# A two-layer hybrid encoder on one core: a compact triangular inversion, group norm by scan step, and 512-column products in the feed-forward's output

## Chip, cores and metric

The kernel runs on 1 core of one Trainium2 chip. The metric is the device time of one execution in microseconds (us); lower is better. Engines are named as in the profile: PE (TensorE, with PEld its weight loads), DVE (VectorE), ACT (ScalarE), POOL (GpSimd) and SP (the engine that issues nearly all DMAs).

## The reference

An encoder of two layers over 256 tokens of width 1024, everything in float32. Each layer:

```python
for l in range(DEPTH):
    h = modulate(rmsnorm(x, norm_gains[l, 0]), sh1, sc1)
    x = x + 0.5 * gt1[:, None, :] * swiglu(h, ffn_wi[l, 0], ffn_wo[l, 0])
    h = modulate(rmsnorm(x, norm_gains[l, 1]), sh2, sc2)
    x = x + gt2[:, None, :] * hybrid_mixer(h, ...)
    h = modulate(rmsnorm(x, norm_gains[l, 2]), sh3, sc3)
    x = x + 0.5 * gt3[:, None, :] * swiglu(h, ffn_wi[l, 1], ffn_wo[l, 1])
return rmsnorm(x, final_norm)
```

The feed-forward's inner width is 2816, so its output product has 22 blocks of 128 to sum over. The shift, scale and gate vectors are `cs @ ada_w[l] + ada_b[l]`, a matrix of 1024 x 9216 per layer. The mixer sums three branches, each gated by a sigmoid: A (dilated attention), B (neighbourhood attention) and C, a recurrence with a state of 64 x 64 per head and direction:

```python
def _rwkv_step(state, inp):
    r, w, k, v, a_vec, b_vec = inp
    sa = jnp.einsum("dbhvk,dbhk->dbhv", state, a_vec)
    state = state * w[..., None, :] + sa[..., None] * b_vec[..., None, :] + v[..., None] * k[..., None, :]
    y = jnp.einsum("dbhvk,dbhk->dbhv", state, r)
    return state, y
...
yn = ((y - mean) * lax.rsqrt(var + GN_EPS)) * gn_w + gn_b        # group norm: one group per head and token
return (jnp.sum(yn + bonus, axis=0) * g)                        # the two directions summed, gated
```

## The kernel before

**Dense products.** Activations lie transposed (features on partitions, 256 tokens in the free dimension). Every float32 operand is split into two fp32r parts, hi and lo, and a product is three: hi·hi, hi·lo and lo·hi. `mm3` (lines 417 to 420) issues them for one 128 x 128 weight block, each with 256 columns: L418 (weights hi, activation hi), L419 (weights hi, activation lo), L420 (weights lo, activation hi). `dense` (L460) does that for all blocks of a sum into one half of a PSUM tile `pmain`, of which there are three. Weights arrive as float32 (`wraw`), ACT rounds a quarter of 512 columns to `whi` (L374) and DVE subtracts to get `wlo` (L383). One quarter holds four blocks, so it feeds twelve products, and four quarters can exist at once (`NSPL`).

**The feed-forward** (`ffn`, L784): 22 inner blocks `z` are made, then eight output blocks m, each a sum over 22 blocks: 176 weight blocks, 528 products of 256 columns. DVE adds each output block to x (`residual`, L609), and ACT and DVE prepare the next norm from it.

**The adaLN matrix** is read a block of 128 x 1024 at a time (`araw`) and reduced on DVE (L482), spread over the program; a block that has not landed holds up whatever stands behind it on DVE.

**Branch C** is done in four chunks of 64 tokens per direction: step n takes chunk n of the forward and chunk 3 - n of the backward direction, 8 heads each. For each step, `invert` (L1165) builds the chunk's masked Gram matrices G (`pG`, L1189) and inverts the unit triangular 64 x 64 matrices. `blocks8` (L1261) inverts the 8 x 8 diagonal blocks: it gathers them (L1270 to L1277), spreads them over the partitions by one product (`p`, L1283), runs a substitution of seven pairs of small DVE operations (L1288, L1292), each pair needing the one in front, and writes the result into 64 x 64 blocks (L1295). Two levels then join 8 x 8 to 16 x 16 and 16 x 16 to 32 x 32 blocks. Each level is a product `pX` = G·T (L1213), a copy to SBUF, a product `pT` (L1225), a masked copy on DVE (L1227) and a transpose of all 32 x 32 squares on DVE (`flip`, L1300). Each of these products is 16 matmuls of 64 x 64 with 64 columns. The third level (`corners`, L1258) is 16 matmuls of 32 x 32 that use the array's 32 x 32 tiles by `tile_position`. A plain float32 matmul shows as two records in the profile, so a group of 16 shows as x32.

`values` (L1302) makes the parts that need no inverse, and `scan` (L1352) runs the four steps in turn: `pAS`, `pU` (needs the inverse), `pS1` (the next state) and `pY`. `post` (L1454) is the group norm, the gate and the sum of directions; it is called for a direction and a half of the tokens, so it waits for two scan steps: the first two calls start after step 1, the last two after step 3. It squares (L1463), sums by a product (`pvar`, L1471), takes a root on ACT and a reciprocal on DVE, spreads it by transposes (`pgi`, L1489) and ends in `oC`, the hi and lo parts that branch C's output products read (L1512 to L1518).

**The order** of all engines' instructions is written down by a small list scheduler when the program is built (`Order`, lines 57 to 133). Pieces of work are generators with a priority; `on(engine, cost)` asks for an engine, and all that a generator issues between two such requests stays together on the engine. The main thread issues the dense products in the order of the weights (`ORDER` = "cabAgB", so branch A's output `A`, gates `g`, branch B's output `B`, then branch C's output), and the others go in between. Buffers are counted (`s_big`: 36 tiles of 4 KB per partition). The order is fixed at build time; on the chip an engine waits at an instruction whose operands are not there, and with it everything behind.

## Time and profile before

| | us |
|---|---|
| median of 3 runs | 1536.39 |
| lowest and highest | 1534.38, 1541.68 |
| the profiled execution | 1537.14 |
| its span in the profile | 1535.3 |

| engine | busy us | share of the span | instructions |
|---|---|---|---|
| PE | 1495.0 | 97% | 14470 |
| DVE | 1283.9 | 84% | 2731 |
| ACT | 859.4 | 56% | 1735 |

The profile is of one execution. Busy time of PE counts overlapping matmuls once; a matmul's record lasts longer than the step to the next one, so the pace is read from starts. The stages lie like this in the span: feed-forward 1 of layer 0 to 215 us, mixer to 589, feed-forward 2 to 779, feed-forward 1 of layer 1 to 970, mixer to 1338, feed-forward 2 to 1526, final norm to the end.

### The profile page before, as it was taken

What the parts mean: (1) busy time and instruction counts of PE and PEld (TensorE: products, weight loads), DVE (VectorE), ACT (ScalarE), POOL (GpSimd) and SP (SyncE); (2) the same over time, 40 slices, a digit from 0 to 9 for tenths busy, and PEclk for the clock granted to TensorE, in tenths of its full rate; (3) what the DMA queues carried; (4) which work ended last, traced back from release to release, by engine and by line L of the source; (5) the groups of instructions that cost most, each with busy time, mean ns of one, the idle gap of its engine ahead of it and who ended that gap; (6) DMA issues with size and microseconds to landing.
All of it is one profiled execution on the core that took longest, in us unless ns stands there. A gap on an engine that the chain in (4) does not pass through costs nothing.

```text
span 1535.3 us, 36372 instructions
## 1 busy us (share of the span) xinstructions
PE 1495.0 (97%) x14470; PEld 1424.6 (93%) x14470; DVE 1283.9 (84%) x2731; ACT 859.4 (56%) x1735; POOL 2.3 (0%) x22
## 2 busy tenths in 40 slices
PE   6999999999999989999999999999999998999998
PEld 6999999988888979999999999998888998999997
DVE  8889789989878888988789877899897888898664
ACT  4556466575444447555565545676655445665554
POOL 0000000000000000000000000000000000000000
PEclk9999999999999979999999999999999999999999
DMA  9688775525345645888668886644343456567553
GB/s 343 226 293 277 259 239 188 179 102 172 118 153 166 211 165 188 280 286 271 223 201 273 276 271 222 216 159 161 109 149 102 167 207 234 167 212 267 189 183 124
DMA packets 97377, 315.76 MB, mean 206 GB/s; under 512 B 11572, under 2 KB 23092, under 8 KB 97208
## 3 DMA queue, kind: packets, MB, share of 16 engines
q1 hardware_dynamic: 96920, 313.35, 60.8%
q8 instruction: 113, 1.85, 0.5%
q14 instruction: 56, 0.46, 0.1%
q10 hardware_dynamic: 288, 0.10, 0.0%
HBM read 310.27 MB, written 3.15 MB: 204 GB/s over the span
## 4 chain that ended last, share of the span: by engine, by line
PE 89%; DMA 5%; DVE 3%; issue 1%; SPq 1%; ACT 0%; DVEq 0%; ACTq 0%
PE pmain L418 21%; PE pmain L419 20%; PE pmain L420 20%; DMA araw<-in_ada_w_dram 3%; PE pearly L418 3%; PE pearly L420 2%; PE pearly L419 2%; DVE wlo L383 1%; PE pT L1225 1%; PE pX L1213 1%; PE pS L1568 1%; PE po L1608 1%; PE pfirst L419 1%; PE pmain L1724 1%; PE pfirst L420 1%; PE pfirst L418 1%
## 5 line engine op out<-in xcount | busy, mean ns | idle before, releaser
L374 ACT CAST whi<-wraw 128x512 fp32r<-128x512 f32 x828 | 508.1, 619 | 444.8 <-PE pmain L419 283.2
L383 DVE TENSOR_TENSOR wlo<-wraw,whi 128x512 fp32r<-128x512 f32 x828 | 567.1, 689 | 117.5 <-ACT whi L374 107.8
L418 PE MATMUL pmain<-h,whi 128*128 128x256 f32 x1840 | 530.5, 288 | 0.0
L419 PE MATMUL pmain<-h,whi 128*128 128x256 f32 x1840 | 517.6, 281 | 0.0
L420 PE MATMUL pmain<-h,wlo 128*128 128x256 f32 x1840 | 515.2, 280 | 0.6 <-DVE wlo L383 0.5
L418 PEld LDWEIGHTS pmain<-h,whi 128*128 128x128 f32 x1840 | 345.9, 188 | 13.9 <-issue 7.8
L420 PEld LDWEIGHTS pmain<-h,wlo 128*128 128x128 f32 x1840 | 347.2, 189 | 1.6 <-DVE wlo L383 1.4
L419 PEld LDWEIGHTS pmain<-h,whi 128*128 128x128 f32 x1840 | 346.5, 188 | 1.1 <-issue 0.7
L482 DVE CUSTOM_DVE_ANT_0 araw<-araw,csb 128x1024 f32<-128x1024 f32 x144 | 175.5, 1221 | 47.2 <-DMA araw<-in_ada_w_dram 46.9
L420 PE MATMUL pmain<-z,wlo 128*128 128x256 f32 x704 | 199.1, 283 | 5.6 <-DVE wlo L383 5.6
L419 PE MATMUL pmain<-z,whi 128*128 128x256 f32 x704 | 198.9, 282 | 0.0
L418 PE MATMUL pmain<-z,whi 128*128 128x256 f32 x704 | 198.1, 281 | 0.0
L420 PEld LDWEIGHTS pmain<-z,wlo 128*128 128x128 f32 x704 | 133.3, 189 | 6.8 <-DVE wlo L383 6.8
L418 PEld LDWEIGHTS pmain<-z,whi 128*128 128x128 f32 x704 | 133.3, 189 | 0.0
L419 PEld LDWEIGHTS pmain<-z,whi 128*128 128x128 f32 x704 | 133.3, 189 | 0.0
L418 PE MATMUL pearly<-xh,whi 128*128 128x258 f32 x320 | 91.4, 286 | 0.0
L419 PE MATMUL pearly<-xl,whi 128*128 128x258 f32 x320 | 90.4, 283 | 0.0
L420 PE MATMUL pearly<-xh,wlo 128*128 128x258 f32 x320 | 90.4, 282 | 0.0
L419 PEld LDWEIGHTS pearly<-xl,whi 128*128 128x128 f32 x320 | 60.6, 189 | 0.0
L420 PEld LDWEIGHTS pearly<-xh,wlo 128*128 128x128 f32 x320 | 60.5, 189 | 0.0
L418 PEld LDWEIGHTS pearly<-xh,whi 128*128 128x128 f32 x320 | 60.4, 189 | 0.0
L441 ACT CAST z<-ffz 128x256 fp32r<-128x256 f32 x76 | 30.6, 405 | 39.8 <-DVE ffz L673 39.7
(308 smaller groups left out, 2328.3 us busy)
## 6 DMA issues: line engine op xcount, KB each, us to landing
wraw<-in_ffn_wi_dram SPq DMA_DIRECT2D x160, 512.0 KB, 4.7
araw<-in_ada_w_dram SPq DMA_DIRECT2D x144, 512.0 KB, 6.5
wraw<-in_ffn_wo_dram SPq DMA_DIRECT2D x88, 512.0 KB, 4.6
wraw<-in_w_in_dram SPq DMA_DIRECT2D x78, 512.0 KB, 3.7
wraw<-in_w_gb_dram SPq DMA_DIRECT2D x72, 512.0 KB, 4.0
w0raw<-in_ffn_wi_dram SPq DMA_DIRECT2D x16, 512.0 KB, 10.9
wraw<-in_w_out_dram SPq DMA_DIRECT2D x16, 512.0 KB, 3.7
bt<-in_bt_dram SPq DMA_DIRECT2D x16, 192.0 KB, 4.4
```

Source lines behind the costliest of these rows:

```text
L374: S_.copy(hi, part(q))
L383: V.tensor_tensor(lo, part(q), hi, op=OP.subtract)
L418: P.matmul(o, w[0], xh, start=first, stop=False)
L419: P.matmul(o, w[0], xl, start=False, stop=False)
L420: P.matmul(o, w[1], xh, start=False, stop=last)
L441: S_.copy(self.hi(k), src)
L482: V.tensor_tensor_reduce(out=raw, in0=raw, in1=csb, scale=0.5, scalar=0.0, op0=OP.mult, op1=OP.add, accum_out=modT[l][:, blk:blk + 1])
L1213: P.matmul(px[half(h), d, h // 2], G[h % 2][half(h), d, h // 2, 0:64], T[half(h), d, h // 2], start=True, stop=True)
L1225: P.matmul(pt[half(h), d, h // 2], X[half(h), d, h // 2], TT[half(h), d, h // 2], start=True, stop=True)
L1568: P.matmul(pS[e][:, t], qT[half(e), hp, t * 128:(t + 1) * 128], kT[half(e), hp], start=True, stop=True)
L1608: P.matmul(po[half(e)], vv[:, j, (2 * hp + e) * 64:(2 * hp + e + 1) * 64], pr_[:, 2 * e + j], start=j == 0, stop=j == 1)
L1724: P.matmul(p[t], ha.hi(kk)[:, xs], wh, start=kk == 0, stop=False)
```

## The change

- **Compact blocks.** The two lower levels keep only the 32 x 32 diagonal squares of each 64 x 64 matrix: T, its transpose `Tt` and X are 128 x 256 instead of 128 x 512. A product of a level becomes `squares`: 32 matmuls of 32 x 32 with 32 columns on the four diagonal tiles of the array, instead of 16 of 64 x 64. The copies, masks and transposes of these levels have half the elements. Ahead of the third level two small operations (on ACT or DVE) spread `Tt` back into the 64 x 64 layout.
- **Substitution in one piece.** The gather and the substitution of `blocks8` are requested from DVE as a whole, so nothing is placed between their operations.
- **Group norm by step.** `pY` is copied into a tile of its own step, and `post` is called once per scan step for that step's two chunks. Two calls follow steps 0 and 1; the calls of steps 2 and 3 add their half and finish `oC`.
- **512 columns.** The hi and lo parts of `z` lie side by side, and one matmul with the hi weights streams both (512 columns) into the two halves of `pmain`; the lo weights follow with 256 columns. The halves are added to x one after the other (`residual2`).

```diff
@@ -446,6 +452,26 @@
+    class Pairs(Act):
+        def __init__(self, name, kt):
+            self.t = [big(name, (128, 2, 2, S), F32R) for _ in range(-(-kt // 2))]
+        def both(self, k):
+            return self.t[k // 2][:, k % 2].rearrange("p a b -> p (a b)")
...
@@ -467,6 +493,17 @@
+    def dense2(p, a, kt):
+        for k in range(kt):
+            yield from tl.next()
+            if a.ev[k].t is None or a.ev[k].t > od.cur.t:
+                yield wait(a.ev[k])
+            yield on("PE", MM, 0.0)
+            P.matmul(p, tl.last[0], a.both(k), start=k == 0, stop=False)
+            P.matmul(p[:, 0:256], tl.last[1], a.hi(k), start=False, stop=k == kt - 1)
...
@@ -612,6 +649,11 @@
+    def residual2(m, p, g, st):
+        yield on("DVE", 0.4, 0.0)
+        V.scalar_tensor_tensor(xT[:, m], p[:, 1], g[:, m:m + 1], xT[:, m], op0=OP.mult, op1=OP.add)
+        yield from residual(m, p[:, 0], g, st)
...
@@ -825,8 +867,8 @@
-            yield from dense(p[:, 0], za, NJ)
-            od.spawn(residual(m, p[:, 0], g, nst), 1)
+            yield from dense2(p.rearrange("p a b -> p (a b)"), za, NJ)
+            od.spawn(residual2(m, p, g, nst), 1)
...
@@ -1174,8 +1216,10 @@
-                    tx = big("tx", (128, 2, 2, 4, 64))
-                    T, X = tx[:, 0], tx[:, 1]
+                    tx = big("tx", (128, 1024))
+                    T, Tt, X = (tx[:, o:o + 256].rearrange("p (d h c) -> p d h c", d=2, h=4) for o in (0, 256, 512))
+                    m = tx[:, 512:1024].rearrange("p (d h c) -> p d h c", d=2, h=4)
+                    X2 = tx[:, 768:896].rearrange("p (h c) -> p h c", h=4)
...
@@ -1192,9 +1236,8 @@
-                yield from blocks8(G, X, TT)
-                yield on("DVE", 0.6)
-                flip(T, TT)
+                yield from blocks8(G, m, Tt)
+                flip(T, Tt)
...
@@ -1206,45 +1249,53 @@
-                    px = paux("pX", (128, 2, 4, 64))
+                    px = paux("pX", (128, 2, 4, 32))
-                    for d in range(2):
-                        for h in range(8):
-                            P.matmul(px[half(h), d, h // 2], G[h % 2][half(h), d, h // 2, 0:64], T[half(h), d, h // 2],
-                                     start=True, stop=True)
+                    squares(px, lambda d, i, b, k, c: G[b][k, d, i, c], lambda d, i, k: T[k, d, i])
-                        yield from copy_any(X, px, 512)
+                        yield from copy_any(X, px, 256)
-                        yield from copy_any(halves_(X, 0), halves_(px, 0), 256)
+                        yield from copy_any(halves_(X, 0), halves_(px, 0), 128)
-                    pt = paux("pT", (128, 2, 4, 64))
+                    pt = paux("pT", (128, 2, 4, 32))
-                    for d in range(2):
-                        for h in range(8):
-                            P.matmul(pt[half(h), d, h // 2], X[half(h), d, h // 2], TT[half(h), d, h // 2], start=True, stop=True)
-                    yield on("DVE", 0.335)
-                    V.copy_predicated(halves_(TT, 1), lvl[:, lv].rearrange("p d (x s) -> p d x s", s=w), halves_(pt, 1))
+                    squares(pt, lambda d, i, b, k, c: X[k, d, i], lambda d, i, k: Tt[k, d, i])
+                    yield on("DVE", 0.55)
+                    V.copy_predicated(halves_(Tt, 1), lvc[:, lv].rearrange("p d (x s) -> p d x s", s=w), halves_(pt, 1))
-                    yield on("DVE", 0.6)
-                    flip(T, TT)
+                    flip(T, Tt)
+                for r in range(2):
+                    yield on(("ACT", "DVE"), (0.37, 0.23))
+                    o, x = TT[:, :, :, 32 * r:32 * r + 32], Tt
+                    if od.cur.pick == "ACT":
+                        S_.activation(o, x, AF.Copy, scale=hm[:, r:r + 1])
+                    else:
+                        V.tensor_scalar(o, x, hm[:, r:r + 1], None, op0=OP.mult)
-                corners(px, lambda d, i, b, k, ca, cb: G[b][k, d, i, cb], lambda d, i, k, ca, cb: T[k, d, i, ca], 1)
-                X2 = X[:, 0, :, 0:32]
+                corners(px, lambda d, i, b, k, ca, cb: G[b][k, d, i, cb], lambda d, i, k, ca, cb: T[k, d, i], 1)
-                corners(pt, lambda d, i, b, k, ca, cb: X2[k, i], lambda d, i, k, ca, cb: TT[k, d, i, cb], 0)
+                corners(pt, lambda d, i, b, k, ca, cb: X2[k, i], lambda d, i, k, ca, cb: Tt[k, d, i], 0)
-                V.copy_predicated(skew(TT[:, 0, :, 32:64], TT[:, 1, :, 0:32]), lvl[:, 2].rearrange("p d (x s) -> p d x s", s=32),
+                V.copy_predicated(skew(TT[:, 0, :, 32:64], TT[:, 1, :, 0:32]), lvl.rearrange("p d (x s) -> p d x s", s=32),
+        def squares(p, w, x):
+            for d in range(2):
+                for i in range(4):
+                    for r in range(4):
+                        k, c = slice(32 * r, 32 * r + 32), slice(32 * (r % 2), 32 * (r % 2) + 32)
+                        P.matmul(p[k, d, i], w(d, i, r // 2, k, c), x(d, i, k), start=True, stop=True, tile_position=(32 * r, 32 * r))
...
@@ -1264,16 +1315,14 @@
+            yield on("DVE", 2.54)
-                yield on("DVE", 0.6, 0.0)
-            yield on("DVE", 0.74)
-            yield on("DVE", 0.6)
...
@@ -1282,18 +1331,16 @@
+            yield on("DVE", 3.2)
-                yield on("DVE", 0.13, 0.13)
-                yield on("DVE", 0.13, 0.13)
-            yield on("DVE", 0.6)
-            V.tensor_mul(by_k(TT), flat(tc8)[:, :, None, :].to_broadcast([128, 8, 8, 8]),
-                         m8[:, None, :, None].to_broadcast([128, 8, 8, 8]))
+            V.tensor_mul(TT.rearrange("p d h (k t) -> p (d h) k t", k=4), flat(tc8)[:, :, None, :].to_broadcast([128, 8, 4, 8]),
+                         m4[:, None, :, None].to_broadcast([128, 8, 4, 8]))
...
@@ -1407,12 +1454,11 @@
-                for d in range(2):
-                    yield from copy_any(RKV[d, 2][:, :, toks(cs[d])], p[:, d], 256)
-                    if n % 2 == 1:
-                        od.set(e_y[d, cs[d] // 2])
+                YS[n] = (W1, TT)
+                yield from copy_any(W1, p, 512)
-                free_big(5 - (n == 3))
+                od.set(e_y[n])
+                free_big(4 - (n == 3))
...
@@ -1451,53 +1497,45 @@
-        def post(d, t):
-            last = d != t
-            ts = slice(t * 128, (t + 1) * 128)
-            yield wait(e_y[d, t])
-            y = RKV[d, 2][:, :, ts]
-            sq = small2("gsq", (128, 4, 128))
+        def post(n):
+            last = n > 1
+            ts = [toks(n), toks(3 - n)]
+            both = lambda t: skew(t[:, :, ts[0]], t[:, :, ts[1]])
+            yield wait(e_y[n])
+            y, sq = YS[n]
+            sqt = sq.rearrange("p d h t -> p (d h t)").rearrange("p (h d t) -> p h d t", h=4, d=2)
+            S_.activation(sqt.rearrange("p h d t -> p d h t"), y, AF.Square)
+            flat = sqt.rearrange("p h d t -> p h (d t)")
+            yield on("PE", 0.9)
+                P.matmul(p[:, 2 * hp:2 * hp + 2], flat[:, hp], sel[:, 0, 0:2], start=True, stop=True)
-                V.tensor_mul(y, y, G1[0][:, :, ts])
+            yield on("DVE", 0.6)
+            V.tensor_mul(y, y, both(G1[0]))
+            yield on("DVE", 0.43)
+            V.tensor_copy(flat.rearrange("p a (b c) -> p (a b) c", b=2), r[:, :, None].to_broadcast([128, 8, 64]))
+            p = paux("pgi", (128, 4, 2, 64))
+            yield on("PE", 0.5)
+                P.transpose(p[:, hp].rearrange("p d t -> p (d t)"), flat[:, hp], ident)
+            pd = p.rearrange("p h d t -> p d h t")
+            b = both(bon[0])
+                yield on("DVE", 1.2)
+                V.tensor_mul(y, y, pd)
+                V.tensor_add(b, b, y)
-                V.tensor_mul(y, y, G1[0][:, :, ts])
+                od.set(e_z[n])
@@ -1505,25 +1543,26 @@
+                yield wait(e_z[3 - n])
+                h, lo = both(oC[0].h[0]), both(oC[0].l[0])
+                    yield on("DVE", 0.67)
+                    V.tensor_mul(y[:, :, sl], y[:, :, sl], pd[:, :, sl])
+                    V.tensor_add(y[:, :, sl], y[:, :, sl], b[:, :, sl])
+                    yield on("ACT", 0.264)
+                    S_.copy(h[:, :, sl], y[:, :, sl])
+                    V.tensor_tensor(lo[:, :, sl], y[:, :, sl], h[:, :, sl], op=OP.subtract)
+            free_big()
-                free_big(4)
+                free_big(2)
...
@@ -1664,9 +1703,8 @@
-            for d in range(2):
-                for t in range(2):
-                    od.spawn(post(d, t), 3)
+            for n in range(4):
+                od.spawn(post(n), 3)
```

Three places show how this moves instructions.

PE, at the end of layer 0's mixer (pY is the scan's last step, pvar and pgi the group norm, o is branch B's attention output, oC branch C's). Before:

```order
L420 MATMUL pmain<-o,wlo 128x256
L1471 MATMUL pvar<-c_sel,gsq 128x2 x8
L1489 MATMUL pgi<-c_ident,gsq 128x128 x8
L418 MATMUL pmain<-oC,whi 128x256
L419 MATMUL pmain<-oC,whi 128x256
```

Now:

```order
L1530 MATMUL pgi<-c_ident,tw 128x128 x4
L424 MATMUL pmain<-h,whi 128x256
L425 MATMUL pmain<-h,whi 128x256
L426 MATMUL pmain<-h,wlo 128x256
...
L426 MATMUL pmain<-o,wlo 128x256
L424 MATMUL pmain<-oC,whi 128x256
```

The first product of oC stood right behind the last pgi; now 102 dense products of 256 columns stand between them in layer 0, and 222 in layer 1 (before: 30 between the last two pgi groups, none behind the last). The last pvar and pgi are half as many.

PE, the third inversion of layer 1 (p is the spreading product of `blocks8`, pX the first level's product that needs the substitution's result). Before, from p on:

```order
L1283 MATMUL p_16392<-tx,c_b_115 128x512
L1378 MATMUL pU<-tw 64x64 x16
L418 MATMUL pmain<-h,whi 128x256
...
L1390 MATMUL pS_16449<-uv,bu 64x64 x16
```

Now, up to pX and behind it:

```order
L1332 MATMUL p_16227<-tx,c_b_118 128x512
L1417 MATMUL pAS<-st,ar 64x64 x16
L424 MATMUL pmain<-h,whi 128x256
...
L1298 MATMUL pX<-tx,G 32x32 x32
L1425 MATMUL pU<-tw 64x64 x16
L1298 MATMUL pT<-tx 32x32 x32
```

Before, pX of this step came after 66 dense products, pU, pS, pY, both pG groups and pvar; now pAS and 9 dense products stand between p and pX, and the scan's pU, pS and pY come between the levels.

DVE, the same inversion (w is the substitution's tile, araw the adaLN blocks). Before:

```order
L1288 TENSOR_TENSOR w_16316<-p_16392,w_16316 128x8x7
L1380 COPY uv<-pU 64x8x64
L1292 TENSOR_TENSOR w_16316<-w_16316 128x2x4x7
L383 TENSOR_TENSOR wlo<-wraw,whi 128x512
L1288 TENSOR_TENSOR w_16316<-p_16392,w_16316 128x8x6
L482 ISA araw,modT_124<-araw,csb 128x1024
```

Now:

```order
L389 TENSOR_TENSOR wlo<-wraw,whi 128x512
L519 ISA araw,modT_127<-araw,csb 128x1024
...
L1337 TENSOR_TENSOR w_16166<-p_16227,w_16166 128x8x7
L1340 TENSOR_TENSOR w_16166<-w_16166 128x2x4x7
...
L1340 TENSOR_TENSOR w_16166<-w_16166 128x2x4
L1342 TENSOR_TENSOR tx<-w_16166,m_113 128x256
L1347 STREAM_TRANSPOSE tx<-tx 128x256
```

The substitution no longer shares DVE with weight splits and adaLN blocks; here two adaLN blocks stand between the last wlo and it.

## Rows read from the trace of the kernel before

**Rows 1.** The page's busy time by engine: busy us, share, instructions.
```profile
PE 1495.0 (97%) x14470; PEld 1424.6 (93%) x14470; DVE 1283.9 (84%) x2731; ACT 859.4 (56%) x1735; POOL 2.3 (0%) x22
```
**Rows 2.** The page's chain that ended last, by engine.
```profile
PE 89%; DMA 5%; DVE 3%; issue 1%; SPq 1%; ACT 0%; DVEq 0%; ACTq 0%
```
**Rows 3.** The page's groups: count | busy, mean ns | idle before, releaser.
```profile
L374 ACT CAST whi<-wraw 128x512 fp32r<-128x512 f32 x828 | 508.1, 619 | 444.8 <-PE pmain L419 283.2
L383 DVE TENSOR_TENSOR wlo<-wraw,whi 128x512 fp32r<-128x512 f32 x828 | 567.1, 689 | 117.5 <-ACT whi L374 107.8
L420 PE MATMUL pmain<-z,wlo 128*128 128x256 f32 x704 | 199.1, 283 | 5.6 <-DVE wlo L383 5.6
```
**Rows 4.** Windows: us, PE, PEld, DVE, ACT, POOL busy (records), granted clock, DMA share, GB/s.
```profile
410.90:539.20 128.30, 127.32 (x2220) 114.81 (x2220) 106.79 (x227) 57.84 (x119) 0.00 (x0) 1.00 0.52 171
539.20:566.40 27.20, 19.91 (x123) 18.33 (x122) 21.92 (x52) 11.01 (x23) 0.00 (x0) 0.69 0.43 151
1155.80:1294.30 138.50, 138.42 (x2320) 126.14 (x2319) 112.05 (x241) 68.45 (x134) 0.00 (x0) 1.00 0.50 170
1294.30:1314.70 20.40, 15.62 (x103) 14.40 (x102) 19.32 (x47) 8.77 (x19) 0.00 (x0) 0.83 0.59 202
146.70:215.20 68.50, 65.07 (x531) 64.67 (x529) 55.16 (x105) 34.32 (x63) 0.93 (x7) 0.98 0.78 264
1463.30:1526.20 62.90, 62.90 (x532) 62.90 (x530) 34.57 (x59) 32.87 (x59) 0.00 (x0) 1.00 0.47 159
```
**Rows 5.** PE in time order, layer 0's mixer end: start, us, what, [idle <-releaser].
```profile
544.75 1.97 PE L1489 MATMUL pgi<-c_ident,gsq 128*128 128x128 f32 x8 [3.25 <-DVE gsq L1484]
550.11 0.58 PE L418 MATMUL pmain<-oC,whi 128*128 128x256 f32 x1 [3.40 <-ACT oC L1516]
```
**Rows 6.** PE in time order: pvar of an earlier half, full clock.
```profile
475.71 1.95 PE L1471 MATMUL pvar<-c_sel,gsq 128*128 128x2 f32 x16
```
**Rows 7.** PE in time order, layer 1's mixer end.
```profile
1294.68 0.66 PE L1489 MATMUL pgi<-c_ident,gsq 128*128 128x128 f32 x4 [0.17 <-DVE gsq L1484]
1296.74 0.38 PE L418 MATMUL pmain<-oC,whi 128*128 128x256 f32 x1 [1.41 <-ACT oC L1516]
```
**Rows 8.** PE: a third-level and a second-level group, the next group; L1258's records.
```profile
422.87 0.45 PE L1258 MATMUL pX<-tx,G 32*32 32x32 f32 x32
423.25 1.15 PE L1225 MATMUL pT<-tw,tx 64*64 64x64 f32 x32
424.33 0.45 PE L1258 MATMUL pT<-tw,tx 32*32 32x32 f32 x32
...
L1258 PE MATMUL pX<-tx,G x256: 191/191/212, 422.9 to 1271.2; 32*32 32x32 f32 x128
```
**Rows 9.** PE in time order: nine products of 512 columns (attention's values).
```profile
299.76 0.40 PE L1724 MATMUL pmain<-whi,h 128*128 128x512 f32 x1
...
301.87 0.28 PE L418 MATMUL pmain<-h,whi 128*128 128x256 f32 x1
```
**Rows 10.** Groups by line on DVE and ACT, columns as in rows 3.
```profile
L482 DVE CUSTOM_DVE_ANT_0 araw<-araw,csb 128x1024 f32<-128x1024 f32 x144 | 175.5, 1221 | 47.2 <-DMA araw<-in_ada_w_dram 46.9
L609 DVE SCALAR_TENSOR_TENSOR xT<-pmain,g,xT 128x256 f32<-128x256 f32 x48 | 23.1, 482 | 14.8 <-PE pmain L420 14.7
L443 DVE TENSOR_TENSOR z<-ffz,z 128x256 fp32r<-128x256 f32 x76 | 31.8, 421 | 1.8 <-ACT z L441 1.8
L1274 DVE TENSOR_REDUCE w<-tx 128x64 f32<-128x512 f32 x8 | 9.0, 1129 | 0.0
L1288 DVE TENSOR_TENSOR w<-p,w 128x56 f32<-128x56 f32 (+6 forms) x56 | 10.2, 187 | 0.3
L1380 DVE COPY uv<-pU 64x512 f32<-64x512 f32 x8 | 5.4, 674 | 1.0 <-PE pU L1378 0.9
L1382 ACT COPY uv<-pU 64x512 f32<-64x512 f32 x8 | 4.7, 582 | 7.0 <-DVE uv L1380 6.9
```
**Rows 11.** The chain that ended last, its end.
```profile
1526.34 0.49 DVE xT L609
```

More of the change, by code (lines that the diff above doesn't have):

```diff
@@ L273, in trunk @@
     sinT = const.tile([128, S], F32, name="sinT")
-    lvl = const.tile([128, 3, 2, 128], U8, name="lvl")
+    lvl = const.tile([128, 2, 128], U8, name="lvl")
+    lvc = const.tile([128, 2, 2, 64], U8, name="lvc")
+    m4, hm = (const.tile([128, n], F32, name=name) for n, name in ((4, "m4"), (2, "hm")))
     bsel = const.tile([128, 2, 2, 128], F32R, name="bsel")
@@ L447, in free, with hi, lo @@
             free_big(2 * self.n)
+    class Pairs(Act):
+        def __init__(self, name, kt):
+            self.n = -(-kt // 4)
+            self.t = [big(name, (128, 2, 2, S), F32R) for _ in range(-(-kt // 2))]
+            self.ev = [Event() for _ in range(kt)]
+        def hi(self, k):
+            return self.t[k // 2][:, k % 2, 0]
+        def lo(self, k):
+            return self.t[k // 2][:, k % 2, 1]
+        def both(self, k):
+            return self.t[k // 2][:, k % 2].rearrange("p a b -> p (a b)")
+        def free(self):
+            free_big(len(self.t))
     class Early:
@@ L469, in dense @@
             mm3(p, tl.last, a.hi(k), a.lo(k), k == 0, k == kt - 1)
+            tl.done()
+    def dense2(p, a, kt):
[6 more added lines that the diff above has]
+            P.matmul(p[:, 0:256], tl.last[1], a.hi(k), start=False, stop=k == kt - 1)
             tl.done()
@@ L763, in first_products @@
             if k == KT - 1:
-                yield take(s_big, 12)
-                za = Act("z", NJ)
+                yield take(s_big, 11)
+                za = Pairs("z", NJ)
             for i in range(NJ0 // 2):
@@ L795, in ffn @@
             od.spawn(modulated(l, n, st, ha), 0)
-            yield take(s_big, 12)
-            za = Act("z", NJ)
+            yield take(s_big, 11)
+            za = Pairs("z", NJ)
         for j in range(j0, NJ):
@@ L1347, in values @@
             if n_val[0] == 4:
-                free_big(4)
-        e_y = {(d, t): Event() for d in range(2) for t in range(2)}
+                free_big(6)
+        e_y, YS = [Event() for _ in range(4)], {}
         def scan():
@@ L1523, in post @@
                 od.release(s_px)
+            free_big()
             n_post[0] -= 1
             if n_post[0] == 0:
-                free_big(4)
+                free_big(2)
         half_done = [0] * 4
```

40 lines of the change are left out of this document (6 added, 34 removed).

## The prediction

> **What bounds the kernel now.** I read the busy times first [rows 1]: PE is busy for 97% of the span, DVE for 84%. PE's figure counts overlapping records, so it doesn't prove that PE is the limit. The chain of waits does [rows 2]: 89% of the path that ended last is PE work, 5% DMA, 3% DVE. The groups agree [rows 3]: before it rounds weights, ACT sat idle 444.8 us, 283.2 of it until PE's dense products gave a buffer back. Weights are prepared faster than PE eats them, so a us taken from PE's work is a us of the span, as long as DVE keeps up.
>
> Then I looked where PE does not work. The windows [rows 4] show both mixers full and at the full clock until branch C's output product (127.3 of 128.3 us busy in layer 0, all of 138.5 in layer 1), and then two holes. From the last product of branch B to the first of w_out PE has 27.2 us in layer 0, with a granted clock of 0.69, and 20.4 us in layer 1, with 0.83. In time order [rows 5] the hole of layer 0 is the group norm: pgi only at 544.75 after 3.25 us idle, oC at 550.11 after 3.40 us idle. PE has nothing else left there. In layer 1 the same happens between pgi and oC [rows 7].
>
> The executed time is 1537.1 us for a span of 1535.3 us; the median of the runs is 1536.4. I sum against 1537.1 and take the 0.7 us off at the end.
>
> **The group norm by step.** The products stay as many: 16 pvar and 8 pgi records in the hole of layer 0, 4 pgi records in that of layer 1, 96 products of oC in each. At the full clock 16 pvar records take 1.95 us from first start to last end [rows 6]; the eight pgi records took 1.97 at half clock, so 1.0 at full [rows 5], and four half of that; a dense product takes 62.9 / 530 = 0.119 us in the last feed-forward's output [rows 4], so 96 take 11.4. Work in the hole of layer 0: 1.95 + 1.0 + 11.4 = 14.4 of 27.2, so **12.8 us** are idle or half clock; in layer 1 0.5 + 11.4 = 11.9 of 20.4, so **8.5 us**. Now the last group norm needs one step's half, and the order puts 102 dense products (12.1 us) in layer 0 and 222 (26 us) in layer 1 between the last pgi and oC. What must happen under that cover is what took from pgi's start to oC's before, 550.11 - 544.75 = 5.4 us for two steps' tokens, with an adaLN block of 1.22 in it [rows 5, 10]. I take all of it: **-21.3 us**. Bounds: with a late DVE a third could remain (-14); more than -21.3 isn't there.
>
> **The compact levels.** Per layer four inversions with two levels of two products: 32 groups in all. A 64 x 64 group takes 424.33 - 423.25 = 1.08 us of PE, a third-level group of 32 records 0.38 to the next group's start [rows 8]. The changed group has 64 records of that third-level kind. Doubling gives 0.76. But of the 0.38 us some is paid once: from first start to last end are 0.45 us, and a record lasts 0.191, so 31 steps take 0.26 and one 8.4 ns, and 0.38 - 0.26 = 0.12 are paid once; 64 records then take 0.54 + 0.12 = 0.66 us. I take 0.66, since the group is not broken: 32 x 0.42 = **-13.4 us**; bounds -10.2 (0.76) and -14.5.
>
> On this the page "TensorEngine Tiling (Array Packing)" of the Trainium skill, Restrictions and Gotchas, speaks against the change: row tiles must not write one PSUM bank at the same time. The rows show otherwise: corner groups on four row tiles write one tile of PSUM at 8 ns a record, so I go by them and keep the rule as a rival.
>
> **512 columns.** 704 weight blocks: three products of 0.119 us become one of 512 and one of 256 columns. Nine products with 512 columns take 301.87 - 299.76 = 2.11 us, 0.234 each [rows 9], against 0.237 for two short ones: 704 x 0.004 = **-2.7 us**; bounds 0 (time goes by columns alone) and -4. The 32 added `residual2` operations cost DVE 0.48 us each [rows 10], 3.9 us in each of four calls. DVE has 28 us free in the last call and 13 in the first [rows 4], so they hide; the three later norms get their first seven blocks first, which is 21 dense products or 2.5 us of cover for a chain that grows by one, from three operations of about 0.48 to four, 1.9 us. Only the very last, in front of the final norm, is on the path [rows 11]: **+0.5 us**. The 5.6 us that PE waits for weights in these stages [rows 3] come from adaLN blocks that land late; they stay, between -4 and +3.
>
> **DVE's smaller operations.** The 24 transposes, eight writes and 16 masked copies are halved, and four spreading operations are added (12 more on ACT); a 256-element operation takes 0.42 us where one of 512 takes 0.69 [rows 3, 10]. That is some 9 us less, beside PE's work: nothing of the sum. If that cover goes, DVE's load in the mixers decides (below).
>
> **New waits.** Since the chain of inversions runs ahead, dense work moves from between its links to its end. Two kinds of links lose cover. First, the spreading product to the first level's product. DVE needs 14 x 0.187 for the substitution, 0.42 for the write and about 0.43 for the transpose: 3.5 us, and in layer 1's third inversion two adaLN blocks of 1.22 stand in front: 5.9 us [rows 10]. PE has pAS (1.08, as the group of the same shape [rows 8]) and 9 dense products (1.07): it waits about **3.5 us**. The other seven have 4.4 to 5.3 us of other work behind the product, about what DVE needs with a weight split or copy in front; I take **+2 us** for them, bounds 0 and +10. Second, in the first step pU to pS: the copies take 0.67 on DVE and then 0.58 on ACT, which waits for DVE's [rows 10]; four pbon products (about 0.5, as four pgi) stand in between where 12 dense ones stood: 0.7 us in each layer, **+1.4 us**. Bounds of all: 0 and +14.
>
> **Sum:** 1537.1 - 21.3 - 13.4 - 2.7 + 0.5 + 3.5 + 2.0 + 1.4 = 1507.1, less 0.7: **1506 us**.
>
> **Rivals.**
>
> *The hole moves into the chain.* PE waits at all eight substitutions as long as at the third of layer 1: 8 x 3.5 = 28 instead of 5.5, so 1506 + 22.5 = 1528.5 us. For it: the order has a stretch in each layer, between branch A's last output and step 0's pY, of about 12 us without steady dense work, and the clock fell to half wherever PE stood still [rows 4]. Against it: in that stretch the small products of other heads and attention stand between the links, and PE was full in the same place before. Chance 0.10.
>
> *Substitution starves the weights (slower).* While DVE gathers (three operations of 512 elements at 0.69 as wlo's, a reduction of 1.13 and a small one of 0.19: 3.4 us [rows 3, 10]) or substitutes (14 x 0.187 + 0.42 = 3.0 us) no wlo is made. A quarter lasts PE 12 x 0.119 = 1.42 us. With three ready quarters in front nothing happens; the point from which it decides is fewer than three. With none ready, all eight inversions cost up to 6.4 us: 51 us, and 1506 + 51 - 5.5 = 1551 us; with one ready 1531. Against it: ACT is kept waiting by full buffers [rows 3], and DVE has 22 us to spare in the last part of layer 0's mixer and 26 in layer 1's [rows 4]. For it: removing 7 us of PE's work per layer and both holes takes that spare time to some 15. Chance 0.04.
>
> *Row tiles take turns (slower).* If a burst of four diagonal tiles that now takes 4 x 8 = 32 ns went one after the other, 64 records would take 64 x 32 ns = 2.05 us, with the end 2.17 instead of 0.66: 32 x 1.51 = 48 us, so 1554 us. The corner groups show that it isn't so [rows 8]. Chance 0.01.
>
> *The tail stays a third* (oC held up by DVE work that the order put in front): 1513 us. It is inside the likeliest case.
>
> **How the numbers follow.** The likeliest case, chance 0.85, runs from 1494 (no new waits, 512 columns at -4, feed-forward stalls gone: 1506 - 6.9 - 1.3 - 4) to 1518 (waits at +14, a part of the tail left). For 8 in 10 I reach a little into the first rival: **1493 to 1525 us**. About 0.5% (7.7 us) can be told from no change, so faster means below 1528.7. The likeliest case is faster throughout; the first rival ends at that border, half of it on each side; the last two are slower. Faster 0.90, same 0.05, slower 0.05.
>
> **What would show it.** Right: oC starts without idle in both layers and the granted clock is 1.00 there; a squares group takes about 0.66 us from start to next start; the 512-column product steps at about 0.234 us; DVE's group L1337/L1340 lies closely packed. Wrong: PE idle in front of pX or pU beyond 7 us in total with releaser DVE (first rival), PE idle in front of dense products with releaser wlo inside the mixers (second), squares groups above 1.1 us (third). If the mixers aren't some 14 us shorter in layer 0 and 9 in layer 1, my reading of the holes was wrong.

## The result, and the profile of the changed kernel

The changed kernel takes 1544.3 us (median of 20 runs, 1533.07 to 1551.68), the kernel before 1536.07 (20 runs, 1533.36 to 1541.68). The ratio is 1.0051 with a 95% interval of 1.0036 to 1.0066: slower by half a per cent, where 1506 us (1493 to 1525) was forecast. The profiled execution, 1551.62 us with a span of 1549.8, lies at the upper end of the runs, 7.3 us above their median.

The page of the changed kernel: busy time by engine, the chain by engine, and the two groups of 512-column output products.

```profile
PE 1491.7 (96%) x14790; PEld 1388.6 (90%) x14790; DVE 1295.7 (84%) x2773; ACT 869.1 (56%) x1745; POOL 2.3 (0%) x22
...
PE 84%; DVE 7%; DMA 5%; issue 3%; ACT 1%; SPq 0%; DVEq 0%; ACTq 0%
...
L505 PE MATMUL pmain<-z,whi 128*128 128x512 f32 x704 | 248.7, 396 | 0.0
L506 PE MATMUL pmain<-z,wlo 128*128 128x256 f32 x704 | 199.3, 283 | 5.3 <-DVE wlo L389 5.3
```

Against [rows 1, 2], PE has 320 records more and 3.3 us less busy time, in a span that is 14.5 us longer. In the chain DVE has grown from 3% to 7% and "issue" from 1% to 3%: time in which the engine waited for nothing that the profile shows.

Where the time lies is told by windows over each mixer, from its first product of h to the next feed-forward's first product (columns as in [rows 4]). First the kernel before:

```profile
239.45:589.23 349.78, 341.21 (x3835) 307.46 (x3834) 305.78 (x674) 194.36 (x425) 0.00 (x0) 0.98 0.48 160
993.93:1337.55 343.62, 338.76 (x3835) 305.75 (x3833) 302.83 (x672) 198.77 (x428) 0.00 (x0) 0.99 0.49 163
```

Then the changed kernel: both mixers, and the 96 products of oC in each layer.

```profile
238.87:588.47 349.60, 338.34 (x4347) 304.78 (x4345) 303.00 (x677) 199.18 (x428) 0.00 (x0) 0.98 0.48 160
997.13:1351.66 354.53, 338.30 (x4347) 305.11 (x4345) 305.58 (x681) 201.11 (x430) 0.00 (x0) 0.97 0.47 157
...
551.90:563.30 11.40, 11.40 (x99) 11.40 (x99) 11.08 (x26) 6.47 (x13) 0.00 (x0) 1.00 0.87 289
1317.00:1328.30 11.30, 11.30 (x99) 11.30 (x98) 10.80 (x24) 6.60 (x13) 0.00 (x0) 1.00 0.82 278
```

The hole at the end is gone in both layers, as forecast: oC runs without idle at a granted clock of 1.00, where [rows 4] had 0.69 and 0.83. But layer 0's mixer is as long as before and layer 1's 11 us longer. What the tail gave was lost earlier in the same mixer, and with it the clock: TensorE was granted half its clock in 41.0 us of the two mixers, against 23.9 us before. PE's waits in the changed kernel name it (line, releaser: us in total, times, longest):

```profile
PE pT L1298 <- issue: 3.8, 2, 3.4
...
PE pX L1298 <- DVE tx L1347: 3.6, 3, 3.2
PE pgi L1530 <- DVE tw L1525: 3.5, 1, 3.5
...
PE pS L1437 <- issue: 3.0, 1, 3.0
PE pvt L1378 <- issue: 2.6, 1, 2.6
...
PE pBT L1369 <- issue: 2.1, 1, 2.1
...
PE pY L1452 <- issue: 1.3, 2, 0.9
...
PE pX L1298 <- issue: 1.1, 1, 1.1
```

With two smaller rows the waits put down to "issue" sum to 15.2 us, in ten stalls; before, there was one:

```profile
PE pU L1378 <- issue: 0.3, 1, 0.3
```

All ten lie in the middle of groups of equal products, not in front of them, which speaks against a late operand. One of them in time order (columns as in [rows 5]):

```profile
463.42 0.75 PE L1298 MATMUL pX<-tx,G 32*32 32x32 f32 x64
464.10 0.38 PE L424 MATMUL pmain<-h,whi 128*128 128x256 f32 x1
464.32 0.28 PE L425 MATMUL pmain<-h,whi 128*128 128x256 f32 x1
464.44 0.28 PE L426 MATMUL pmain<-h,wlo 128*128 128x256 f32 x1
464.64 0.56 PE L1437 MATMUL pS<-uv,bu 128*64 128x64 f32 x10
468.18 0.86 PE L1437 MATMUL pS<-uv,bu 128*64 128x64 f32 x22 [2.98 <-issue]
```

Ten records of pS run, then PE stands for 2.98 us, then the other 22 run. An undisturbed compact group is here too: 464.10 - 463.42 = 0.68 us (0.66 forecast).

What PE lacked is its instructions. The page lists two queues of the kind "instruction"; the one that fits PE's number of instructions is

```profile
q8 instruction: 116, 1.90, 0.5%
```

116 packets of 16,384 bytes. PE's records are 14,790 products and as many weight loads, with 76 others 29,656, and 116 x 256 = 29,696: so a packet is a block of 256 instructions of PE. Read from the trace's packets (times in the span), around that stall and in a stretch of dense products:

```
block  fetch starts  lands    PE instructions started since block x 256
30        448.48     449.42   206
31        457.79     458.72   185
32        465.85     466.80   449
33        470.70     471.72   375
45        570.10     570.97   188
46        586.53     587.46   193
```

In the dense stretch PE has started some 190 instructions of its present block when the next fetch starts, and it uses a block in 16 us, so a fetch of 1 us is hidden. Around 465 us PE used 520 instructions between two fetches, 8.1 us apart, and stood at 449 until the next block had landed (466.80, next record 468.18). All ten "issue" stalls of this kernel stood at exactly 449, whatever the product: in pU, pvt, pBT, pS and pY, in compact groups and in a third-level group. So did the single one of the kernel before, in a 64x64 group. So, from the point where a fetch usually starts, PE has fewer than 300 instructions left.

The fetch itself came late there. In the four stalls of over 2 us (3.0, 2.6, 2.1 and 3.4) the fetch that PE stood for started 5.7 to 8.1 us after the one before it, while the DMA engines were busy for 75% or more of the 2 us ahead of its start. That these transfers delay it is likely, but no run varied them.

The Trainium skill ("Runtime: NRT & Kernel Launch", Instruction fetch mechanics) says that instructions are refilled in 16 KiB blocks of 256 and that crossing a block is mostly hidden; the block's size agrees with the trace, "hidden" holds for the dense stretch alone.

**Theory F**, formed from this: a float32 product is four instructions here (two records, two weight loads). A 64x64 group is 64 instructions in 1.08 us, a compact group 128 in 0.68. Where groups crowd, compact ones ask for instructions faster than they come. **Rival S**: my first rival of before, the chain of inversions waits for DVE. **Rival R**: the loss belongs to the 32x32 tiles or the compact layout itself.

### The profile page after: what moved, and what is told of

It is laid out like the page before. It is cut to its first block, busy times and chain, and to the rows that moved or that the text cites. A ratio compares the mean times of both kernels' runs of the same rounds, so it can differ in the third digit from the quotient of the medians.

```text
span 1549.8 us, 37072 instructions
## 1 busy us (share of the span) xinstructions
PE 1491.7 (96%) x14790; PEld 1388.6 (90%) x14790; DVE 1295.7 (84%) x2773; ACT 869.1 (56%) x1745; POOL 2.3 (0%) x22
## 4 chain that ended last, share of the span: by engine, by line
PE 84%; DVE 7%; DMA 5%; issue 3%; ACT 1%; SPq 0%; DVEq 0%; ACTq 0%
PE pmain L424 16%; PE pmain L426 15%; PE pmain L425 15%; PE pmain L505 9%; PE pmain L506 5%; DMA araw<-in_ada_w_dram 3%; PE pearly L424 2%; PE pearly L425 2%; PE pearly L426 2%; DVE wlo L389 2%; PE pfirst L425 1%; PE pmain L1762 1%; PE pfirst L426 1%; PE pPT L1638 1%; PE pfirst L424 1%
## 5 line engine op out<-in xcount | busy, mean ns | idle before, releaser
L505 PE MATMUL pmain<-z,whi 128*128 128x512 f32 x704 | 248.7, 396 | 0.0
L505 PEld LDWEIGHTS pmain<-z,whi 128*128 128x128 f32 x704 | 132.9, 189 | 30.7
L424 PE MATMUL pfirst<-h,w0h 128*128 128x256 f32 x128 | 36.7, 287 | 3.2 <-ACT h L787 3.2
L424 PE MATMUL pmain<-o,whi 128*128 128x256 f32 x128 | 38.3, 299 | 0.0
## 6 DMA issues: line engine op xcount, KB each, us to landing
w0raw<-in_ffn_wi_dram SPq DMA_DIRECT2D x16, 512.0 KB, 10.9
```

The costliest lines, as they stand in the source:

```text
L424: P.matmul(o, w[0], xh, start=first, stop=False)
L505: P.matmul(p, tl.last[0], a.both(k), start=k == 0, stop=False)
```

## Experiments

**1. The change without its compact levels.** `invert` keeps its 64x64 products; all else is as changed.

```diff
-  squares(px, lambda d, i, b, k, c: G[b][k, d, i, c], lambda d, i, k: T[k, d, i])
+  for d in range(2):
+      for h in range(8):
+          P.matmul(px[half(h), d, h // 2], G[h % 2][half(h), d, h // 2, 0:64], T[half(h), d, h // 2], ...)
```

> The change without the compact levels: the two lower levels are 64x64 products again, all else (substitution in one piece, group norm by step, 512 columns) as changed. The order of PE now has 99 and 111 dense products between the last pgi and the first oC product. Theory F (PE runs out of instructions: a block of 16 KB, 256 instructions, is fetched about a block ahead, and groups of 32x32 products use one up in 1.3 us): 64x64 groups use 59 instructions per us instead of 194, so idle of PE in the middle of a group (releaser 'issue') falls from some 13 us to below 2, half-clock stretches inside the mixers go, and the time is 1514 to 1524 us. Rival S (the chain of inversion waits for DVE, my first rival): the substitution is still in one piece, the idle before pX and pgi stays and the time stays at 1535 to 1545.

Measured: 1521.13 us, ratio 0.9914 (0.9886 to 0.9941). The two mixers are 24 us shorter than the changed kernel's:

```profile
237.29:577.31 340.02, 333.96 (x3835) 302.96 (x3833) 307.62 (x676) 200.30 (x426) 0.00 (x0) 1.00 0.49 165
976.97:1317.17 340.20, 334.68 (x3834) 303.33 (x3833) 309.16 (x681) 197.83 (x422) 0.00 (x0) 0.99 0.49 164
```

Idle time of PE (span less busy) is 11.6 us instead of 27.5; the stretches at half clock inside the mixers, 41.0 us in the changed kernel, are 3.4 us. "Issue" waits sum to 0.4. This is what F said, and it beats both kernels. But the order of the instructions is another one here, so F is not yet shown alone. A further 9.0 us of difference between the two profiled executions lie between the mixers, 4.6 of them in the first 14 us behind layer 0's mixer; no run explains these.

**2. The compact levels alone** on the kernel before (edit: the reverse of the above, without the other parts).

> The kernel before with the compact levels alone (substitution placed piece by piece, old group norm, 256 columns). F: PE stands in the middle of groups, 5 to 15 us in total, the clock falls to half behind the longer ones, and the hole at the end of the mixers stays: 1535 to 1550 us. S: without the piece of DVE work the links wait for nothing, the shorter groups give their 13 us: 1520 to 1526.

Measured: 1555.97 us, ratio 1.0138 (1.0116 to 1.0161), a little beyond F's range and far from S's. Its longest waits in the middle of groups:

```profile
PE pT L1262 <- issue: 4.3, 3, 2.1
...
PE pvt L1346 <- issue: 3.2, 1, 3.2
...
PE pX L1262 <- issue: 2.8, 2, 2.4
PE pX L1273 <- issue: 2.4, 1, 2.4
PE pMV L1356 <- issue: 2.2, 1, 2.2
```

**3. Group norm by step and 512 columns alone** (as 1, and the substitution's operations requested one by one as before).

> The change without the compact levels and with the substitution placed piece by piece: group norm by step and 512 columns alone. In its order no dense product stands between the last pgi and oC, so the hole stays in part, with half the group norm in it: F and S both 1522 to 1534 us, no idle in the middle of groups. If it is as fast as the run without compact levels, the substitution in one piece is worth nothing.

Measured: 1539.88 us, ratio 1.0035 (1.0021 to 1.0049): above the range. There is no idle in the middle of groups, but the order has no cover for the tail, and pgi (4.5 us), pU (3.9), oC (2.8), pvar (2.7) and pY (2.5) wait for DVE or ACT. So in the order that it gets by itself the group norm by step gains nothing; run 1 has dense work left for the end, and this one has not.

**4. The price of the instructions by itself:** three bursts of small products in the feed-forwards of the kernel before.

```diff
+  p = paux("pburst")
+  for g in range(20):
+      for i in range(32):
+          k, o = slice(32 * (i % 4), 32 * (i % 4) + 32), c * (i // 4) % 512
+          P.matmul(p[k, o:o + c], ident[k, k], ident[k, 0:c], start=True, stop=True, tile_position=(k.start, k.start))
```

> The kernel before with three bursts of 20 groups of small products on a constant that nobody waits for, behind the inner blocks of a feed-forward: 16 products of 64x64 with 64 columns (layer 0, second), 32 of 32x32 with 32 columns (layer 1, first), 32 of 32x32 with 128 columns (layer 1, second). F: the first takes about 22 us (1280 instructions, one block in 4.3 us); the second has 2560 instructions and is bound by fetching, 10 blocks at 2.5 to 4 us each, so 25 to 40 us, with idle at each block; the third the same 25 to 40. Rival (a product of this shape is not bound by its instructions): the second takes 20 x 0.66 = 13 us without idle.

Measured (one execution, 1641.88 us), PE in time order, first the 64x64 burst, then 32x32 with 32 columns, then with 128:

```profile
718.77 4.58 PE L846 MATMUL pburst<-c_ident 64*64 64x64 f32 x149
723.55 3.94 PE L846 MATMUL pburst<-c_ident 64*64 64x64 f32 x128 [0.19 <-issue]
731.94 13.53 PE L846 MATMUL pburst<-c_ident 64*64 64x64 f32 x363 [4.45 <-issue]
...
940.26 1.93 PE L850 MATMUL pburst<-c_ident 32*32 32x32 f32 x128 [4.31 <-issue]
946.75 1.93 PE L850 MATMUL pburst<-c_ident 32*32 32x32 f32 x128 [4.56 <-issue]
950.49 1.93 PE L850 MATMUL pburst<-c_ident 32*32 32x32 f32 x128 [1.82 <-issue]
954.51 1.93 PE L850 MATMUL pburst<-c_ident 32*32 32x32 f32 x128 [2.09 <-issue]
958.25 1.93 PE L850 MATMUL pburst<-c_ident 32*32 32x32 f32 x128 [1.81 <-issue]
...
973.51 0.74 PE L850 MATMUL pburst<-c_ident 32*32 32x32 f32 x37 [1.54 <-issue]
...
1532.38 35.92 PE L850 MATMUL pburst<-c_ident 32*32 32x128 f32 x1280
```

In the 32-column burst PE stops after every 128 records, which are 256 instructions: one block. From 946.75 to 958.25 three blocks take 11.5 us, 3.8 each, so 67 instructions in a us. The 20 groups take 40 us (933.91 to 974.18), 2.0 each: F, not 13 us. The clock is not the reason: it was halved from 939.3 us on, but ten blocks of 1.93 us are only 19 us. The pace holds where little else is moved: from 946.75 us on the DMA engines are 2% busy. The two stops of 4.31 and 4.56 us before that, and the 4.45 us of the 64x64 burst, fell where they were busy for 85% or more of the 2 us ahead of the fetch, and there the fetches started 8.6, 6.6 and 8.3 us apart. The 64x64 burst needs a block in 3.9 us at full clock and took 26.6 us in all, against the forecast of 22. The third burst ran 1280 records in 35.9 us at full clock, without idle that is listed; at 3.6 us a block it lies at the pace itself. It uses the same 32x32 tiles and as many instructions as the second, so the tiles by themselves don't stop PE (against R). A compact group therefore costs 0.68 us where instructions are in store and an estimated 1.9 where they are not (128 at 67 in a us); a 64x64 group, whose 64 instructions take 0.95 at that pace, stays at 1.08 unless the fetch is delayed.

**5. Twice the instructions without 32x32 tiles:** run 1 with each product of 64 columns in two halves.

```diff
-  P.matmul(px[half(h), d, h // 2], G[...], T[half(h), d, h // 2], ...)
+  for c in (slice(0, 32), slice(32, 64)):
+      P.matmul(px[half(h), d, h // 2, c], G[...], T[half(h), d, h // 2, c], ...)
```

> The run without compact levels, with each 64x64 product of 64 columns cut into two of 32 columns: the same columns in total, the same order of all engines, twice the instructions (128 in a group, as the compact one has). F: fetching 256 instructions takes 3.4 to 4.0 us as in the burst, so the stalls come back without any 32x32 tile: idle in the middle of groups 8 to 20 us, time 1535 to 1550 us against 1521. Rival R (the loss belongs to the 32x32 tiles or the compact blocks): within 5 us of 1521.

Measured: 1554.66 us, ratio 1.0113 (1.0089 to 1.0136). It lies above F's range, but not for F's reason: no "issue" waits are listed in the mixers, and each group simply lasts longer, 2.08 us for 64 records:

```profile
406.62 2.08 PE L1250 MATMUL pX<-tx,G 64*64 64x32 f32 x64
409.88 2.08 PE L1263 MATMUL pT<-tw,tx 64*64 64x32 f32 x64
```

From start to next start it is 2.00 instead of 1.08, and 32 x 0.92 = 29 of the 33.5 us. A 64x64 record costs 31 ns with 32 columns and 34 with 64. At 64 instructions in a us it stays under the pace, so the run does not tell F from R: I had not asked what such a record costs with half the columns. One wait, 2.0 us in pvar of layer 1, is put down to ACT, but there too PE stood at 449 until a block had landed.

**6. Half the instructions in the same order:** the whole change, with the 16 products of one direction in each compact group replaced by one 128x128 product. The inverse of the backward direction is left out.

```diff
 def squares(p, w, x):
-    for d in range(2):
+    P.matmul(p[:, 1], ident, x(1, slice(0, 4), slice(0, 128)), start=True, stop=True)
+    for d in range(1):
```

> The whole change, but in each group of compact products the 16 of the backward direction are replaced by one product of 128x128 with 128 columns on a constant (the inverse of that direction is left out): the order, DVE's and ACT's work and PE's busy time stay about the same, the instructions of a group fall from 128 to 68. F: the idle in the middle of groups falls below 3 us and the time to 1512 to 1526 us. S and R: the chain waits as before, 1538 to 1545.

Measured: 1524.14 us, ratio 0.9913 (0.9899 to 0.9928), 20 us below the changed kernel, with the same order and the same operations on DVE and ACT. A group takes about 0.76 us, a little more than the compact one. PE's waits:

```profile
PE pgi L1531 <- DVE tw L1526: 3.5, 1, 3.5
PE pX L1294 <- DVE tx L1348: 3.4, 3, 3.0
...
PE pT L1310 <- issue: 1.6, 2, 0.8
```

"Issue" waits fall from 15.2 us to 2.2; the waits for DVE in the chain stay within 0.2 us of what they were. This is F, and it rules out S for those 20 us. The run halves the 32x32 products together with the instructions, so R is ruled out by other traces: by the third burst of run 4, and by PE standing at 449 in groups of every shape, in the kernel before as well.

What is left in run 6's mixers:

```profile
237.75:574.96 337.21, 333.35 (x3867) 300.01 (x3865) 303.22 (x678) 199.66 (x430) 0.00 (x0) 0.99 0.50 166
977.74:1324.05 346.31, 336.90 (x3866) 303.12 (x3865) 305.16 (x681) 200.92 (x430) 0.00 (x0) 0.97 0.49 161
```

PE is idle for 13.3 us, close to run 1's 11.6, but its clock is halved for 27.3 us, where run 1 has 3.4.

**7. One piece alone:** the kernel before with one request for the gather (2.54) and one for the substitution (3.2).

> The kernel before with the substitution in one piece and nothing else. The group-norm run without it was 1540 and with it 1521, so the piece seems to be worth 19 us there, by a chain that runs ahead and leaves dense work for the end: here the order has 3 and 138 dense products between the last pgi and oC, so layer 1's hole of 8.5 us goes and layer 0's stays: 1524 to 1531 us. If the piece only works together with the group norm by step: 1533 to 1538.

Measured: 1532.28 us, ratio 0.9969 (0.9957 to 0.9981), 1 us above the first range and below the second. With run 3 it suggests that the two parts work together, each in the order that the planner gave it: by the ratios -5 us for the piece alone, +5 for the group norm alone (run 3), -13 together (run 1), 512 columns in the latter two.

**8. 512 columns alone.**

> The kernel before with 512 columns in the feed-forward's output and nothing else: 704 x 0.004 = 2.7 us less and 0.5 more, so 1531 to 1536 us; if the time goes by columns alone, 1536.

Measured: 1535.13 us, ratio 0.9989 (0.9976 to 1.0002): as forecast, and too little to be told from nothing.

**9. More instructions in the same order:** run 1 with 32 dummy products ahead of each 64x64 group of the two lower levels.

```diff
+  for i in range(32):
+      k = slice(32 * (i % 4), 32 * (i % 4) + 32)
+      P.matmul(px[k, i // 16, i // 4 % 4, 0:32], ident[k, k], ident[k, 0:32], start=True, stop=True, tile_position=(k.start, k.start))
```

> The run without compact levels, with 32 small products (32x32, on a constant, overwritten at once) put in front of each 64x64 group of the two lower levels: 128 instructions and 0.54 us of PE more in each of 32 groups, everything else and its order the same. By PE's work alone (rival): 1521 + 17 = 1538 us, no idle in the middle of groups. F: 192 instructions in 1.62 us are more than the 65 to 75 per us that are fetched, so PE also stands in the middle of groups (5 to 25 us with the clock): 1545 to 1565 us.

Measured: 1575.43 us, ratio 1.0257 (1.0235 to 1.0279), 54 us above run 1 and 10 above F's range. An undisturbed pair of dummies and group takes 1.76 us, so the work is 32 x 0.68 = 22 us. "Issue" waits, next to none in run 1, are now 21:

```profile
PE pT L1265 <- issue: 6.2, 5, 3.7
PE pX L1253 <- issue: 5.3, 2, 2.7
...
PE pT L1269 <- issue: 3.9, 5, 1.7
```

Of the rest, some 11 us, at most 8.5 are the clock, which is halved for 20.5 us of the mixers instead of 3.4. Each "issue" stall stands at 449 again, one of them among dense products. The stalls come with the instructions, although nobody waits for what the dummies compute.

**10 to 12. Run 1 in other orders**, by the planner's costs alone: 1.9 us for every 64x64 group (0.85 in the code, 1.08 on the chip), then 2.5, then 3.6 instead of 3.2 for the substitution.

> The run without compact levels, with a planner cost of 1.9 us instead of 0.85 for the 64x64 groups (1.0 instead of 0.5 for corners): nothing but the order changes. It has 159 and 174 dense products behind the last pgi, and at most 196 small products for 30 dense ones instead of 348. If the waits of 5.5 us before pX come from links placed too closely, they shrink: 1510 to 1520 us; if they come from DVE's own queue, 1519 to 1524.

> The same with a planner cost of 2.5 us (1.3 for corners): 138 and 120 dense products behind the last pgi, at most 152 small products for 30 dense ones. 1508 to 1520 us, or 1519 to 1524 as above.

> The run without compact levels, with the substitution's cost in the planner at 3.6 us instead of 3.2: it took 3.8 us of DVE in that run (first product at 410.44, write from 413.61 for 0.6) and PE waited 2.8 us twice in front of the first level's product. Nothing but the order changes: 111 and 138 dense products behind the last pgi. If the cost was what placed the link too closely, both waits shrink by the 0.4 us or go: 1514 to 1520 us; if DVE's queue ahead of the substitution sets them, 1519 to 1526 as before. No theory of the compact levels hangs on it.

Measured: 1565.6 us (ratio 1.0200, 1.0174 to 1.0226), 1569.05 (1.0230, 1.0205 to 1.0255) and 1541.33 (1.0027, 1.0013 to 1.0041). All three miss their ranges, and on the wrong side. In the first, PE's waits for DVE have grown:

```profile
PE pX L1249 <- DVE tx L1332: 16.9, 13, 2.7
PE p L1317 <- DVE tx L1311: 7.2, 6, 2.7
```

In run 1 the same two were 5.5 and 1.6 us. A likely reason, not tested: a planner that believes a group to last 1.9 us counts it as cover for DVE's work, and 0.8 us of that cover isn't there on the chip. What the runs do show is that the order alone moves this kernel by 17 to 48 us (by the ratios to run 1), as much as any part of the change or more.

## Why the prediction was wrong

**The compact levels: the step that failed.** I sized a compact group from the third level's records, 0.66 us, and wrote -13.4 us. Undisturbed it is 0.68, so the size of the work was right; the price of its instructions was missing. I carried over a rate that I had seen in groups of 32 records, between dense work, onto stretches where groups of 64 records follow each other. Runs 4 and 6 put it in place: at 3.8 us a block, removing half of the instructions in the same order gives back 20 us. Against run 1 the compact levels cost 21 us by the ratios (1.0051 and 0.9914) instead of gaining 13; there the order is part of the difference. The 3.8 us are the pace with little else moved; at the four longest stalls of the changed kernel the fetches came 5.7 to 8.1 us apart.

None of my rivals said this. The rule of the Trainium skill that I weighed ("TensorEngine Tiling (Array Packing)", Restrictions and Gotchas) is not what happened: 64 records on four row tiles, into one tile of PSUM, took 0.68 us. I looked at how fast the array takes small products, and not at how fast it is given them, though the numbers were in the trace: 14,470 records of PE and as many of its weight loads [rows 1], in blocks whose fetches started as close as 3.7 us in the mixers before, where PE already stood once at 449.

**The hole at the end** (-21.3): right in place and mechanism, since oC starts behind dense work in both layers at full clock. Run 1, which is the change without its compact levels, was by my terms 1506 + 13.4 = 1519.4 us; it took 1521.1 (1522.9 by its ratio). So the sum of all other terms held within 2 to 4 us in that order. Part of this may be luck: runs 10 to 12 are the same instructions in other orders and take 17 to 48 us more. The last sign that I named, mixers shorter by 14 and 9 us, failed (0.2 shorter and 10.9 longer) and would have blamed the holes, which were read rightly.

**512 columns** (-2.7 and +0.5): -1.7 us by the ratio of run 8, with an interval of -3.7 to +0.3; in the changed kernel a 512-column product steps at 0.232 us, where I had 0.234. Right, within what can be told.

**New waits** (+6.9): the second step that failed, since I priced the idle time and put the clock that it costs at nothing. The idle time itself was about right: waits of branch C's chain for DVE and ACT sum to 9.1 us (pX 3.6, pgi 3.5, p 1.4, pS 0.6), within my bounds. The third inversion of layer 1 waited 3.2 us for DVE, where I had 3.5 (3.8 by my own figures: 5.9 less 1.08 and 1.07), and pS for uv's second half 0.6, where I had 1.4. Not foreseen were pgi of layer 1's first step (3.5 us) and what each stall does to the clock:

```profile
460.00:470.00 10.00, 7.02 (x272) 6.23 (x273) 6.39 (x13) 2.09 (x5) 0.00 (x0) 0.98 0.77 245
470.00:480.00 10.00, 10.00 (x190) 9.09 (x190) 7.56 (x15) 3.94 (x9) 0.00 (x0) 0.85 0.27 86
500.00:510.00 10.00, 8.30 (x256) 7.38 (x249) 7.65 (x17) 2.79 (x6) 0.00 (x0) 1.00 0.78 286
510.00:520.00 10.00, 8.64 (x134) 7.84 (x134) 3.33 (x8) 3.91 (x6) 0.00 (x0) 0.53 0.20 75
```

After the stall of 2.98 us the next 10 us ran at 0.85, after that of 2.64 at 0.53. Counted over both mixers against run 1: 23.9 us more in all, of which 15.9 are idle, and PE is busy 8.0 us longer although its groups are 32 x 0.40 = 12.8 us shorter. So some 21 us are work that ran longer. The 37.6 us more at half clock (41.0 - 3.4) can account for at most half their length, 18.8 us, and are the only cause that I see. Run 6 adds up the same way: PE is busy 1.6 us longer than in run 1 although its groups are 32 x 0.32 = 10.2 us shorter, together 11.8, and half of 27.3 - 3.4 is 12.0.

**The first rival** (the hole moves into the chain, 1528.5 us, chance 0.10) was right in direction only: its sign, more than 7 us of idle in front of pX or pU with DVE as releaser, didn't come (3.6). In run 6, with the shortage nearly gone, the time is 1524, some 15 us above my sum for it (1506, and 32 x 0.1 for its longer groups); by the count above most of that is clock and not idle time. (The 1531 us of the second rival are 1529 by its own figures, which changes nothing.)

The chance of 0.90 for faster rested on the belief that every cost of the change was in view; the term with the steepest extrapolation should have had a bound on the other side of zero, as a price that the trace does not show.

## What to carry to other kernels

Count instructions as well as work: when a product is cut into smaller tiles, compare its instructions per us with the pace at which the queue of instructions was seen to refill them (here 256 in 3.8 us for PE with little else moved, in 5.7 to 8.6 us where the DMA engines were 75% busy or more), and look whether several such groups follow each other. A stall in the middle of a group of equal products, with "issue" as its releaser, was no dependency here: each time PE stood at the same instruction of a block until the next block had landed. Price a stall with the clock that follows it, as the trace shows it, and not by its idle time alone. With an order that is planned at build time, test a part of a change with the order held fixed; here the order alone was worth as much as the parts or more.

## What the runs showed of the hardware

- PE was given 256 instructions in 3.4 to 4.1 us when it had run dry and little else was moved (run 4), though the packet itself took 0.9 to 1.1 us; it always ran dry at the same point, some 290 instructions after the earliest point at which a fetch started (160 to 449 into a block).
- A float32 product of 64x64 took 31 ns a record with 32 columns (run 5) and 34 with 64, so cutting its columns from 64 to 32 saved a tenth; 32x32 products with 32 columns on four diagonal tiles took 8.4 ns a record, into one PSUM tile.
- The runs of the changed kernel spread over 18.6 us (1533.07 to 1551.68), those of the kernel before over 8.3. In both kernels, the time from PE's 160th instruction of a block to the start of the next fetch was longer where other transfers filled over 80% of the DMA engines in the 2 us ahead of it (median 2.1 us) than where they filled under 10% (0.8 and 1.1 us). That chance in these transfers spreads the runs is likely, but not tested.
